# Order of the recurrence's activations, place of one projection, and the first two weights' loading in a two-layer trunk

## The chip, the cores and the metric

The kernel runs on one core of a Trainium2 chip. The metric is the time of one execution on the device, in microseconds. The engines of the core work side by side, each through its own queue in order: TensorE (PE; its weight loads PEld), VectorE (DVE), ScalarE (ACT), GpSimd (POOL), and SyncE (SP), which issues the transfers.

## What is computed

A trunk of two layers over 1024 latent tokens (x) and 256 context tokens, 1024 channels wide. The change touches the first layer only: its modulated input, the recurrence (RG-LRU) and the neighbouring gating unit. In the reference:

```python
shift, scale, gate = modulation(c, w_mod[l], b_mod[l])
h = x * (1.0 + scale) + shift
p = h @ w_in                       # five branches of 512 channels
xl = depthwise_conv(p[..., :W], conv_w, conv_b)
...
gate_r = sigmoid(einsum(xh, w_a) + b_a)      # for each of two directions
gate_i = sigmoid(einsum(xh, w_x) + b_x)
log_a = (-LRU_C * gate_r) * softplus(-lam)
a = exp(log_a)
bterm = sqrt(-expm1(2.0 * log_a)) * (gate_i * xc)
h_lat = linear_scan(a, b, forward) + linear_scan(a, b, reverse)
...
y_a = h_rec * silu(p[..., W:2 * W])
u = gelu(p[..., 2 * W:3 * W])
v = gelu(p[..., 3 * W:4 * W])
y_b = spatial_gating(u, v, ...) * silu(p[..., 4 * W:5 * W])
```

Everything is float32. Each matrix product is made of three matmuls on a high part and a low part of both operands: high by high, high by low, low by high.

## The kernel before

**Layout.** Channels lie on the partitions, tokens along the free dimension: 256 context and 1024 latent tokens, 1280 columns, in chunks of 256, 512 and 512. A weight tile has 128 output channels and eight blocks of 128 input channels. `wload` (line 143) fetches it into `wraw` (two buffers) and makes it into two halves of four blocks: `whi`, a ScalarE copy (L138), and `wlo`, a subtraction (L141), on GpSimd unless another engine is named; `whi` and `wlo` have four buffers each.

**The front (lines 264 to 338).** In eight steps of 128 input channels, `load0` fetches a block of x (640 KB) and of the modulation's weights (1 MB), four buffers each; `mod0` computes the modulation on TensorE (`modp`, L221), `hmod` transposes it (L298), scales x on VectorE (L307) and splits it into high parts (`hhc` for context, `hhl` for latents, L309, ScalarE) and low parts (`hlc`, `hll`, L312 and L313, VectorE). In between, step by step, TensorE advances two projections: `px` (weight 0, the recurrence's input of tile 0) and `pg` (weight 4, its gate branch), nine matmuls per step each (L164). The first four steps use the first half of each weight, the last four the second.

**The recurrence (lines 344 to 516).** The 512 channels of the recurrence are four tiles f = 0 to 3. For each: `lru_x` projects (`px`), evacuates it on ScalarE (`xp`, L363 and L364), convolves on VectorE (L367 and L369) and splits the result (`xh`, `xo`); `lru_g` projects (`pg`), takes a tanh on ScalarE (`sg`, L382) and multiplies on VectorE (L383), which reads `pg` in PSUM too; `lru_rec` computes four gates, two for each direction d, nine matmuls each (`pgate`, L399 to L401), a tanh of each (`gt`, L403: r, then x), a second tanh on r (`tt`, L407), Exp (L408), and four VectorE passes (L409 to L412); `lru_scan` takes Sqrt on ScalarE (L421), multiplies (L424), scans (L426 to L432), adds and gates (L438, L439) and stores the tile. The order of the calls is x0, g0, x1, then rec0 with scan0, g1, x2, rec1 with scan1, g2, x3, rec2 with scan2, g3, the u projection (`pu`, weight 8, with a Gelu into `ut0`, L513), rec3, the rest of the modulation blocks, and after that scan3, the z projection (`pz`, L530 and L531), a second u projection and the v tiles (`pv`, L208).

**PSUM.** All projections and gates take tiles of three banks from one tag with two buffers (`pj3`, line 260). A tile can therefore start only when all readers of the one before the last are done: for `px` that is ScalarE, for a gate its tanh, for `pg` the tanh and L383, for `pu` the Gelu, for `pz` L531.

**Order.** TensorE runs in program order. On the other engines a planner places the instructions: at each moment, of those that are ready, the one that comes first in the program. In the front, SyncE too runs in program order. `mod_step` (line 484) is called at several places; each third call does one block of modulation work (`mod_do`: 16 matmuls, a VectorE copy of its result, and, of the block before, a transpose or a gate row).

Of the kernel before, what the change touches and what calls it, by code (L numbers as in the profile page):

```python
# [10 lines left out]
F32 = mybir.dt.float32  # L11
F32R = mybir.dt.float32r
# [30 lines left out]
def tile_hybrid_trunk(es: ExitStack, tc: tile.TileContext, A, out, scr=None):  # L43
    nc = tc.nc
    V, S, G, T, SY = nc.vector, nc.scalar, nc.gpsimd, nc.tensor, nc.sync

    def pool(name, space=None, **kw):
        if space is not None:
            kw["space"] = space
        return tc.tile_pool(name=name, bufs=1, reuse_waits="tile", **kw)  # L50

    def f32(ap):
        return ap.bitcast(F32)
# [3 lines left out]
    wp = es.enter_context(pool("w"))  # L57
# [71 lines left out]
    def hs(c0, n):  # L129
        if c0 < CTX:  # L130
            return hhc[:, :, c0:c0 + n], hlc[:, :, c0:c0 + n]
        return hhl[:, :, c0 - CTX:c0 - CTX + n], hll[:, :, c0 - CTX:c0 - CTX + n]

    def split(hi, lo, src, he=None, le=None):
        he = he or S
        le = le or V
        if he is S:
            S.activation(hi, src, AF.Copy)  # L138
        else:
            he.tensor_copy(hi, src)  # L140
        le.tensor_tensor(lo, src, f32(hi), op=ALU.subtract)  # L141

    def wload(src, nk=8, le=None):
        raw = wp.tile([128, nk, 128], F32, name="wraw", tag="wraw", bufs=2)
        SY.dma_start(raw, src)
        res = []
        for h in range(nk // 4):
            hi = wp.tile([128, 4, 128], F32R, name="whi", tag="whi", bufs=4)
            lo = wp.tile([128, 4, 128], F32R, name="wlo", tag="wlo", bufs=4)
            split(hi, lo, raw[:, 4 * h:4 * h + 4], le=le or G)  # L150
            res.append((hi, lo))
        return res
# [5 lines left out]
    def proj3_g(ps, w):  # L158
        outs = [(ps[:, 256 + c0:256 + c0 + n], hs(c0, n)) for c0, n in CHUNKS]
        for k in range(KT):  # L160
            hi, lo = w[k // 4]
            for wt, hx, st, sp_ in ((hi, 0, k == 0, False), (hi, 1, False, False), (lo, 0, False, k == KT - 1)):
                for o, hh in outs:
                    T.matmul(o, wt[:, k % 4], hh[hx][:, k], start=st, stop=sp_)  # L164
            yield 1.63
# [11 lines left out]
    def proj3(ps, w):  # L177
        run(proj3c_g(ps, w))
# [81 lines left out]
    def pj3(name):  # L260
        t = pj.tile([128, 1536], F32, name=name, tag="pj", bufs=2)
        return t

    px0, pg0 = pj3("px"), pj3("pg")
# [8 lines left out]
    def load0(k):  # L273
        wm = stp.tile([128, KT, 256], F32, name="wm0", tag="wm0", bufs=4)
        xt = stp.tile([128, NTOK], F32, name="xt", tag="xt", bufs=4)
        if k:
            SY.dma_start(xt, A["xcT"][128 * k:128 * k + 128])
        if k:
            SY.dma_start(wm, A["w_mod0"][k])
        else:  # L280
            SY.dma_start(wm[:, 0:4], A["w_mod0"][k][:, 0:4])
            SY.dma_start(wm[:, 4:8], A["w_mod0"][k][:, 4:8])
            SY.dma_start(ident, A["ident"])
            SY.dma_start(xt, A["xcT"][128 * k:128 * k + 128])
        WM[k], XT[k] = wm, xt

    def mod0(k):
        p = psb("modp")
        wm = WM.pop(k)
        mod_mm(p[:, 0:256], [wm[:, i] for i in range(KT)], range(KT))  # L290
        mb = stp.tile([128, 256], F32, name="mb0", tag="mb0", bufs=2)
        S.activation(mb, p[:, 0:256], AF.Copy)
        return mb

    def hmod(k, mb):
        p = psb("modcp")
        for i in range(2):
            T.transpose(p[:, 128 * i:128 * i + 128], mb[:, 128 * i:128 * i + 128], ident)  # L298
        t = const.tile([128, 2, 2], F32, name="mct0", tag="mct", bufs=2)
        V.tensor_reduce(t, p[:, 0:256].rearrange("p (i g r) -> p i r g", g=4, r=32)[:, :, 0:2, :], axis=AX.X,  # L300
                        op=ALU.add)
        V.tensor_tensor(modc[:, k], t, bmodc[:, k, :, None].to_broadcast([128, 2, 2]), op=ALU.add)
        xt = XT.pop(k)
        parts = []
        for c0, n, cnd in ((0, 256, 1), (256, 512, 0), (768, 512, 0)):
            x = xt[:, c0:c0 + n]
            V.tensor_scalar(x, x, modc[:, k, 1, cnd:cnd + 1], modc[:, k, 0, cnd:cnd + 1], op0=ALU.mult, op1=ALU.add)  # L307
            hh, hl_ = hs(c0, n)
            S.activation(hh[:, k], x, AF.Copy)  # L309
            parts.append((hl_[:, k], x, f32(hh[:, k])))  # L310
            if len(parts) == 2:
                V.tensor_tensor(*parts.pop(0), op=ALU.subtract)  # L312
        V.tensor_tensor(*parts.pop(0), op=ALU.subtract)  # L313

    so_cm = tc.manual_schedule(engines={nc.sync.engine})
    so_cm.__enter__()
    load0(0)
    gx = proj3_g(px0, wload(A["w_in0"][0]))
    load0(1)
    gg = proj3_g(pg0, wload(A["w_in0"][4]))  # L320
    hmod(0, mod0(0))
    for k in range(KT):
        if k + 2 < KT:
            load0(k + 2)
        if k == 0:
            next(gx)
        if k == 3:
            decay()
        if k + 1 < KT:
            mb = mod0(k + 1)  # L330
        if k:
            next(gx)
        if k + 1 < KT:
            hmod(k + 1, mb)
        next(gg)
# [10 lines left out]
    with pool("lrua") as lp, pool("lruc") as lc:  # L346
        def lt(name, tag, bufs, dt=F32):
            t = {"gr": lb, "gx": lb, "tt": lb, "xl": lc}.get(tag, lp).tile([128, WC], dt, name=name, tag=tag, bufs=bufs)
            return t
# [36 lines left out]
        def lru_rec(f):  # L386
            (wh, wl), = wload(A["wg"][f], nk=4)
            mod_step()
            xl, xh, xo = XL[f]
            bs = []  # L390
            for d in range(2):
                i8 = 4 * d + f
                gts = []
                for g in range(2):
                    p = pj3("pgate")
                    m = 2 * d + g
                    for c0, n in ((0, 258), (258, 512), (770, 512)):
                        o = p[:, 254 + c0:254 + c0 + n]
                        T.matmul(o, wh[:, m], xh[:, c0:c0 + n], start=True, stop=False)  # L399
                        T.matmul(o, wh[:, m], xo[:, c0:c0 + n], start=False, stop=False)  # L400
                        T.matmul(o, wl[:, m], xh[:, c0:c0 + n], start=False, stop=True)  # L401
                    t = lt("gt", "gr" if g == 0 else "gx", 2)
                    S.activation(t, p[:, 254:1536], AF.Tanh, scale=0.5, bias=hb[:, 8 * g + i8:8 * g + i8 + 1])  # L403
                    gts.append(t)
                r, gi = gts
                tt = lt("tt", "tt", 2)
                S.activation(tt, r, AF.Tanh, scale=sp2[:, i8:i8 + 1], bias=sp2[:, i8:i8 + 1])  # L407
                S.activation(r, r, AF.Exp, scale=sn4[:, i8:i8 + 1], bias=sn4[:, i8:i8 + 1])  # L408
                V.scalar_tensor_tensor(gi, gi, 1.0, xl, op0=ALU.add, op1=ALU.mult)  # L409
                V.scalar_tensor_tensor(tt, r, 1.0, tt, op0=ALU.add, op1=ALU.mult)  # L410
                V.tensor_scalar(r, tt, -1.0, 1.0, op0=ALU.mult, op1=ALU.add)
                V.scalar_tensor_tensor(tt, r, 1.0, tt, op0=ALU.add, op1=ALU.mult)  # L412
                bs.append((r, gi, tt))
                mod_step()
            return bs

        def lru_scan(f, bs):
# [36 lines left out]
        def mod_do():  # L454
            if late:
                mod_c(*late.pop(0))
            if pend:
                l, blk, wm = pend.pop(0)
                p = psb("modp")
                mod_mm(p, wm, range(8))  # L460
                mb = lp.tile([128, 512], F32, name="mb", tag="mb", bufs=1)
                V.tensor_copy(mb, p)
                late.append((l, blk, mb))
                mod_load()
# [17 lines left out]
        late, pend, calls = [], [], [0]  # L482

        def mod_step():
            calls[0] += 1
            if calls[0] % 3 == 2:
                mod_do()
# [20 lines left out]
        u0 = u0_cm.__enter__()  # L508
        ut0 = u0.tile([128, NTOK], F32, name="ut0")
        zt0 = u0.tile([128, NTOK], F32, name="zt0")  # L510
        p = pj3("pu")
        proj3(p, wload(A["w_in0"][8]))
        S.activation(ut0, p[:, 256:1536], AF.Gelu_apprx_tanh)  # L513
        rec3 = lru_rec(3)
        while pend or late:
            mod_do()


    vp_cm = pool("sguv", side="right")
# [598 lines left out]
    with pool("out1") as op, pool("po1", PSUM) as po:  # L1118
        rows = []
        for i, nm in enumerate(("ln_g", "ln_b")):  # L1120
            for l in range(2):
                r = op.tile([128, D], F32, name=f"row{nm}{l}")
# [144 lines left out]
```

## Time and profile before

| | |
|---|---|
| median of three runs | 1149.4 us (1149.16 to 1150.6) |
| the profiled execution: its time | 1150.2 us |
| its span, first to last instruction | 1148.4 us |
| TensorE busy | 1122.0 us, 98% of the span |
| VectorE busy | 726.5 us, 63% |
| ScalarE busy | 448.8 us, 39% |
| GpSimd busy | 257.9 us, 22% |

All times in a trace count from the start of the span. In the order of time a line has the start, the duration, engine, source line, operation, output <- inputs, shapes and count; several like instructions in a row are merged (x2). Brackets hold the engine's idle time before it and what ended that. TensorE's matmuls overlap, and their ends are modelled, so that steps from start to start tell more than durations. The line of a helper (L138, L141) stands for whoever called it; the tile's name tells which.

### The profile page before, as it was taken

The numbers are of one execution on the slowest core, as the hardware profiler recorded it, in microseconds if no ns is written. First come the engines' busy times: TensorE is split into PE (matmuls) and PEld (weight loads), VectorE is DVE, ScalarE is ACT, GpSimd is POOL, SyncE is SP. The second block draws the span as 40 slices with busy tenths as digits, with TensorE's granted clock in tenths as the row PEclk, the third lists the DMA queues.
The fourth block names the chain that finished last, engine by engine and source line by source line (L and its number), as shares of the span: only waits on it lengthen the run. The fifth ranks groups of instructions, "written<-read, shape, count | busy, mean of one in ns | idle before, by whom it ended". The sixth has DMA issues, their size and how long they took to land. (4 is left out here: it accounts for less than half of the span.)

```text
span 1148.4 us, 14901 instructions
## 1 busy us (share of the span) xinstructions
PE 1122.0 (98%) x5842; PEld 922.1 (80%) x5842; DVE 726.5 (63%) x1025; ACT 448.8 (39%) x701; POOL 257.9 (22%) x176
## 2 busy tenths in 40 slices
PE   6999999999999999999999999999999999999997
PEld 3777777778888888888888788888888888888786
DVE  4678986943511566646302758876877876738996
ACT  3453755710131233352113545545554554423210
POOL 1022212540140122285301301122211211220021
PEclk9999999999999999999999999999999999999999
DMA  9554543230142544345215312332321410126641
GB/s 372 210 176 172 190 141 132 93 96 1 60 146 75 170 140 136 109 141 168 97 46 144 106 46 69 83 103 64 92 60 38 137 52 20 46 68 240 206 147 74
DMA packets 71093, 133.92 MB, mean 117 GB/s; under 512 B 5856, under 2 KB 34400, under 8 KB 70128
## 3 DMA queue, kind: packets, MB, share of 16 engines
q1 hardware_dynamic: 71024, 132.97, 34.4%
q8 instruction: 46, 0.75, 0.3%
q14 instruction: 23, 0.19, 0.0%
HBM read 105.67 MB, written 27.28 MB: 116 GB/s over the span
## 5 line engine op out<-in xcount | busy, mean ns | idle before, releaser
L141 POOL TENSOR_TENSOR wlo<-wraw,whi 128x512 fp32r<-128x512 f32 x90 | 137.8, 1536 | 561.1 <-ACT whi L138 561.1
L978 DVE TENSOR_REDUCE st<-psc 128x1 f32<-128x1280 f32 x64 | 95.1, 1485 | 36.9 <-PE psc L977 36.8
L661 PE MATMUL pout<-woh,yhi 128*128 128x512 f32 (+1 forms) x296 | 114.8, 388 | 0.3 <-DVE xres L1159 0.3
L663 PE MATMUL pout<-woh,ylo 128*128 128x512 f32 (+1 forms) x296 | 114.4, 386 | 0.3 <-DVE ylo L141 0.3
L980 ACT ACTIVATE e<-psc,st 128x1280 f32<-128x1280 f32 x64 | 85.1, 1330 | 75.1 <-DVE st L978 74.4
L662 PE MATMUL pout<-wol,yhi 128*128 128x512 f32 (+1 forms) x296 | 114.1, 386 | 0.0
L138 ACT ACTIVATE whi<-wraw 128x512 fp32r<-128x512 f32 x92 | 57.2, 628 | 126.3 <-PE px L173 29.0
L184 PE MATMUL p<-hhl,whi 128*128 128x512 f32 x256 | 104.7, 409 | 0.0
L186 PE MATMUL p<-hhl,wlo 128*128 128x512 f32 x256 | 100.6, 393 | 0.0
L185 PE MATMUL p<-hll,whi 128*128 128x512 f32 x256 | 100.3, 392 | 0.0
L976 PE MATMUL psc<-k,qh 128*128 128x512 f32 (+1 forms) x192 | 67.3, 365 | 2.1 <-ACT e L980 2.0
L977 PE MATMUL psc<-k,ql 128*128 128x512 f32 (+1 forms) x192 | 68.7, 358 | 0.0
L138 ACT ACTIVATE ah<-atr 128x512 fp32r<-128x512 f32 (+1 forms) x96 | 46.9, 523 | 50.1 <-PE atr L999 49.5
L661 PEld LDWEIGHTS pout<-woh,yhi 128*128 128x128 f32 x296 | 55.6, 188 | 12.4 <-issue 0.6
L663 PEld LDWEIGHTS pout<-woh,ylo 128*128 128x128 f32 x296 | 55.6, 188 | 12.0 <-DVE ylo L141 0.7
L138 ACT ACTIVATE yhi<-yraw 128x512 fp32r<-128x512 f32 x36 | 22.5, 631 | 109.0 <-PE pout L662 77.4
L662 PEld LDWEIGHTS pout<-wol,yhi 128*128 128x128 f32 x296 | 55.7, 188 | 11.6 <-DVE wol L141 0.2
L141 DVE TENSOR_TENSOR al<-atr,ah 128x512 fp32r<-128x512 f32 (+1 forms) x96 | 54.6, 594 | 6.4 <-ACT ah L138 6.0
L186 PEld LDWEIGHTS p<-hhl,wlo 128*128 128x128 f32 x256 | 48.0, 188 | 10.7
L185 PEld LDWEIGHTS p<-hll,whi 128*128 128x128 f32 x256 | 48.3, 189 | 8.4
L184 PEld LDWEIGHTS p<-hhl,whi 128*128 128x128 f32 x256 | 48.2, 188 | 8.3
L1081 DVE SCALAR_TENSOR_TENSOR e<-e,st 128x1280 f32<-128x1280 f32 x32 | 51.6, 1612 | 0.8
(320 smaller groups left out, 2813.1 us busy)
## 6 DMA issues: line engine op xcount, KB each, us to landing
wraw<-in_w_in_dram SPq DMA_DIRECT2D x44, 512.0 KB, 3.7
wm<-in_w_mod_dram SPq DMA_DIRECT2D x64, 256.0 KB, 4.6
wraw<-in_w_out_dram SPq DMA_DIRECT2D x16, 512.0 KB, 3.5
wm<-in_w_mod_dram SPq DMA_DIRECT2D x7, 1024.0 KB
xt<-in_xcT_dram SPq DMA_DIRECT2D x8, 640.0 KB, 10.1
xres<-in_xc_dram SPq DMA_DIRECT2D x10, 512.0 KB, 3.7
kd<-k_d SPq DMA_DIRECT2D x16, 320.0 KB, 4.8
wvr<-in_w_v_dram SPq DMA_DIRECT2D x8, 512.0 KB, 4.9
```

The lines of the kernel that those rows point to most:

```text
L138: S.activation(hi, src, AF.Copy)
L141: le.tensor_tensor(lo, src, f32(hi), op=ALU.subtract)
L184: T.matmul(o, hi[:, k % 4], hh[:, k], start=k == 0, stop=False)
L185: T.matmul(o, hi[:, k % 4], hl_[:, k], start=False, stop=False)
L186: T.matmul(o, lo[:, k % 4], hh[:, k], start=False, stop=k == KT - 1)
L661: T.matmul(o, hi[:, i], wh[:, c], start=first and i == 0, stop=False)
L662: T.matmul(o, hi[:, i], wl[:, c], start=False, stop=False)
L663: T.matmul(o, lo[:, i], wh[:, c], start=False, stop=not first and i == 3)
L976: T.matmul(o, qh[:, m, cu], KS[m][:, c:c + n], start=True, stop=False)
L977: T.matmul(o, ql[:, m, cu], KS[m][:, c:c + n], start=False, stop=True)
L978: V.tensor_reduce(st[:, m:m + 1], p[:, 256:1536], axis=AX.X, op=ALU.max, negate=True)
L980: S.activation(e_, p[:, 256:1536], AF.Exp, bias=st[:, m:m + 1], scale=1.0, accum_out=st[:, 2 + m:3 + m])
```

## The change

Three edits:

1. In `lru_rec` the four gates of a tile, for both directions, come first, each with its tanh; the second tanh, Exp and VectorE's passes follow for both directions. `mod_step` is called after each direction's gates; the order on TensorE within a tile is the same.
2. The first u projection (weight 8, 72 matmuls, its Gelu) comes after the gates of tile 3 and after the last modulation work, and no longer between g3 and rec3. So rec3 follows g3 directly.
3. The first two weights (0 and 4) are fetched in halves: the first half in the old place, the second half of weight 0 in step 1 and that of weight 4 in step 2. Their low parts are computed on VectorE (the default of `split`), not on GpSimd.

```diff
@@ -314,12 +314,32 @@
 
     so_cm = tc.manual_schedule(engines={nc.sync.engine})
     so_cm.__enter__()
+    def wstart(f):
+        raw = wp.tile([128, 8, 128], F32, name="wraw", tag="wraw", bufs=2)
+        res = []
+
+        def half(h):
+            SY.dma_start(raw[:, 4 * h:4 * h + 4], A["w_in0"][f][:, 4 * h:4 * h + 4])
+            hi = wp.tile([128, 4, 128], F32R, name="whi", tag="whi", bufs=4)
+            lo = wp.tile([128, 4, 128], F32R, name="wlo", tag="wlo", bufs=4)
+            split(hi, lo, raw[:, 4 * h:4 * h + 4])
+            res.append((hi, lo))
+
+        half(0)
+        return res, half
+
     load0(0)
-    gx = proj3_g(px0, wload(A["w_in0"][0]))
+    w0, half0 = wstart(0)
+    gx = proj3_g(px0, w0)
     load0(1)
-    gg = proj3_g(pg0, wload(A["w_in0"][4]))
+    w4, half4 = wstart(4)
+    gg = proj3_g(pg0, w4)
     hmod(0, mod0(0))
     for k in range(KT):
+        if k == 1:
+            half0(1)
+        if k == 2:
+            half4(1)
         if k + 2 < KT:
             load0(k + 2)
         if k == 0:
@@ -387,7 +407,7 @@
             (wh, wl), = wload(A["wg"][f], nk=4)
             mod_step()
             xl, xh, xo = XL[f]
-            bs = []
+            bs, gates2 = [], []
             for d in range(2):
                 i8 = 4 * d + f
                 gts = []
@@ -402,7 +422,11 @@
                     t = lt("gt", "gr" if g == 0 else "gx", 2)
                     S.activation(t, p[:, 254:1536], AF.Tanh, scale=0.5, bias=hb[:, 8 * g + i8:8 * g + i8 + 1])
                     gts.append(t)
-                r, gi = gts
+                gates2.append(gts)
+                mod_step()
+            for d in range(2):
+                i8 = 4 * d + f
+                r, gi = gates2[d]
                 tt = lt("tt", "tt", 2)
                 S.activation(tt, r, AF.Tanh, scale=sp2[:, i8:i8 + 1], bias=sp2[:, i8:i8 + 1])
                 S.activation(r, r, AF.Exp, scale=sn4[:, i8:i8 + 1], bias=sn4[:, i8:i8 + 1])
@@ -411,7 +435,6 @@
                 V.tensor_scalar(r, tt, -1.0, 1.0, op0=ALU.mult, op1=ALU.add)
                 V.scalar_tensor_tensor(tt, r, 1.0, tt, op0=ALU.add, op1=ALU.mult)
                 bs.append((r, gi, tt))
-                mod_step()
             return bs
 
         def lru_scan(f, bs):
@@ -508,12 +531,12 @@
         u0 = u0_cm.__enter__()
         ut0 = u0.tile([128, NTOK], F32, name="ut0")
         zt0 = u0.tile([128, NTOK], F32, name="zt0")
+        rec3 = lru_rec(3)
+        while pend or late:
+            mod_do()
         p = pj3("pu")
         proj3(p, wload(A["w_in0"][8]))
         S.activation(ut0, p[:, 256:1536], AF.Gelu_apprx_tanh)
-        rec3 = lru_rec(3)
-        while pend or late:
-            mod_do()
 
 
     vp_cm = pool("sguv", side="right")
```

## Rows read from the trace of the kernel before

**Rows 1.** The page: busy time, share of the span, instructions of each engine.

```profile
PE 1122.0 (98%) x5842; PEld 922.1 (80%) x5842; DVE 726.5 (63%) x1025; ACT 448.8 (39%) x701; POOL 257.9 (22%) x176
```

**Rows 2.** TensorE's waits: us in total, times, longest.

```profile
PE pgate L399 <- ACT ut L513: 1.3, 1, 1.3
...
PE pgate L399 <- ACT gt L403: 1.0, 2, 0.6
...
PE pv L208 <- DVE zt L531: 0.6, 1, 0.6
...
PE pg L172 <- ACT gt L403: 0.5, 1, 0.5
```

**Rows 3.** Order of time, 10 to 27 us: start, duration, what [idle before].

```profile
10.77 1.13 ACT L138 ACTIVATE whi<-wraw 128x512 fp32r<-128x512 f32 x2
11.24 0.42 DVE L312 TENSOR_TENSOR hlc<-xt,hhc 128x256 fp32r<-128x256 f32 x1
...
11.43 0.58 PE L164 MATMUL px<-hhc,whi 128*128 128x256 f32 x1 [2.04 <-ACT whi L138]
11.46 3.02 POOL L141 TENSOR_TENSOR wlo<-wraw,whi 128x512 fp32r<-128x512 f32 x2 [11.02 <-ACT whi L138]
...
13.26 1.76 DVE L313 TENSOR_TENSOR hll<-xt,hhl 128x512 fp32r<-128x512 f32 x1
...
16.87 1.94 PE L221 MATMUL modp<-wm,csil 128*32 128x256 f32 x16
...
20.01 1.05 PE L164 MATMUL pg<-hhl,whi 128*128 128x512 f32 x2
...
22.62 0.68 DVE L313 TENSOR_TENSOR hll<-xt,hhl 128x512 fp32r<-128x512 f32 x1
...
24.51 0.63 PE L164 MATMUL px<-hhl,whi 128*128 128x512 f32 x2
...
26.55 0.17 DVE L300 TENSOR_REDUCE mct<-modcp 128x4 f32<-128x16 f32 x1 [3.25 <-PE modcp L298]
```

**Rows 4.** Order of time on TensorE around gates, tiles 0 and 3.

```profile
73.11 0.29 PE L399 MATMUL pgate<-xh,whi 128*128 128x258 f32 x1
...
75.00 0.39 PE L399 MATMUL pgate<-xh,whi 128*128 128x258 f32 x1
...
196.91 0.39 PE L401 MATMUL pgate<-xh,wlo 128*128 128x512 f32 x1
198.63 0.39 PE L399 MATMUL pgate<-xh,whi 128*128 128x258 f32 x1 [1.33 <-ACT ut L513]
```

**Rows 5.** Order of time, TensorE and VectorE, where pg ends (three tiles).

```profile
97.64 0.28 PE L172 MATMUL px<-hhc,whi 128*128 128x256 f32 x1
...
102.05 1.46 DVE L383 SCALAR_TENSOR_TENSOR sg<-sg,pg 128x1280 f32<-128x1280 f32 x1
...
140.37 0.28 PE L172 MATMUL px<-hhc,whi 128*128 128x256 f32 x1
...
146.34 1.48 DVE L383 SCALAR_TENSOR_TENSOR sg<-sg,pg 128x1280 f32<-128x1280 f32 x1
...
181.63 0.28 PE L172 MATMUL pu<-hhc,whi 128*128 128x256 f32 x1
...
189.75 1.48 DVE L383 SCALAR_TENSOR_TENSOR sg<-sg,pg 128x1280 f32<-128x1280 f32 x1
```

**Rows 6.** Order of time on ScalarE, recurrence of tile 2.

```profile
159.94 1.47 ACT L407 ACTIVATE tt<-gt,sp 128x1282 f32<-128x1282 f32 x1
161.31 1.31 ACT L403 ACTIVATE gt<-pgate,hb 128x1282 f32<-128x1282 f32 x1
...
172.03 1.28 ACT L408 ACT_TABLE_LOAD   x1
...
182.62 1.28 ACT L421 ACTIVATE tt<-tt 128x1282 f32<-128x1282 f32 x1 [1.76 <-DVE tt L412]
...
185.73 1.24 ACT L382 ACTIVATE sg<-pg 128x1280 f32<-128x1280 f32 x1
```

## The prediction

> **What bounds the kernel now.** I read the page first: TensorE is busy for 98% of the span [rows 1]. Only two things can therefore change the time: idle time of TensorE, and stretches in which it runs slowly. The second view is the list of TensorE's waits [rows 2]. In the parts that the change touches it holds small sums: 1.3 us for a gate's matmuls that wait for the Gelu of the u projection, 1.0 us in two waits for a gate's tanh, 0.5 us for the next projection behind a tanh, 0.6 us for the v tiles behind a VectorE pass. The third view is the order of time in the first 27 us [rows 3]. There TensorE waits and also runs slowly: two 512-column matmuls take 1.05 us at 20.01, but 0.63 us at 24.51. [...] From 24 us on it has hardly a gap. So the whole matter is some 9 us at the front and five small waits in the recurrence.
>
> The matmuls' ends are modelled, so a listed gap is a little short. [...] The loss is 1.72 - 0.23 = 1.49, not the 1.33 of the bracket. I add the same 0.16 to every gap of that kind.
>
> **The front.** Before, ScalarE copies both halves of the first weight, 1.13 us for two, ahead of the latent columns; GpSimd computes both lows in 3.02 us; beside it VectorE's second subtraction (hll) takes 1.76 us, whereas the same pass takes 0.68 us at 22.62 with GpSimd idle [rows 3]. TensorE starts the first projection at 11.43 and reaches the next modulation only at 16.87. After: only one copy stands ahead, so the copies of the latent columns start 0.57 earlier, at 11.25, and the first of them is there at 11.8. VectorE is through with x when hlc starts, at 11.24; then one low (0.68, as the pass of the same size at 22.62), hlc 0.42 and two hll at 0.68 end at about 13.8. TensorE's nine matmuls of the first step need 3 x (0.21 + 2 x 0.427) = 3.2 us from 11.43 on, 0.21 being half of 0.427 for the 256 columns; they wait some 0.3 us for the copy and 0.4 us for the second hll: the modulation at 15.3 instead of 16.87, **-1.6 us**. Ends: -0.6, if only the copy counts, and -2.0, if neither wait is left.
>
> What is put later: the two second halves, each with a transfer, a copy and a VectorE low. The transfers stand on SyncE's queue ahead of what waits for free buffers, and the same bytes come in the end. VectorE idles 3.25 us per step while it waits for the transposes [rows 3], and four lows are 4 x 0.68. I take 0; if that cover failed each time, +2.7. A ScalarE copy whose transfer is late would hold the next modulation's copy behind it on the queue; that lies inside the same bound.
>
> **The tanh ahead.** No instruction is added or removed; the program order of ScalarE changes, and the planner places what is ready. In tile 2 the order was tanh of r, the second tanh on r (159.94), tanh of x (161.31), although x came first in the program too [rows 6]. It filled the time in which the gate's matmuls (75.00 - 73.11 = 1.89 us per gate [rows 4]) were not done. That filler stays ready after the change, so I expect the waits for the x tanh, 1.0 in the list [rows 2], to stay: between 0 and -1.3 with the 0.16 each, taken as 0. Between the third tanh and the second, Exp (L408) no longer has precedence. The next projection waited for that third tanh; its 0.54 + 0.16 goes: **-0.70** (0 if Exp still slips in).
>
> **The u projection behind the last gates.** The matmuls are the same 72, with one weight transfer, two copies, two GpSimd lows and a Gelu. It is moved past a gate weight's transfer, 36 gate matmuls, the last modulation steps, and on SyncE past their small transfers; the weights are fetched two tiles ahead in either order, so I cost the queues at 0. It no longer stands between gates that want its buffer: **-1.49**. The pass that the v tiles waited for (L531) stood behind the last tile's scans on VectorE; these now come a whole projection earlier: 0.62 + 0.16, **-0.78** (0 if the pass stays late). The last modulation's gate row still has two gates' matmuls ahead of it to cover VectorE's copy; if a scan stands in front of that copy, up to +2.4, taken as 0.
>
> **What takes its place.** The projections and gates share two PSUM buffers. The gates of the last tile now follow the pg projection directly. Their first gate takes the other buffer; the second wants pg's own, and this is free only when ScalarE's tanh (sg) and then VectorE's L383 have read it. Before, 72 matmuls of another projection covered that. The rows give the time from the start of the next tile on TensorE to the end of L383 [rows 5]: 102.05 + 1.46 - 97.64 = 5.87; 146.34 + 1.48 - 140.37 = 7.45; and for this very tile 189.75 + 1.48 - 181.63 = 9.60. One gate covers 1.89, so the stall is 3.98, 5.56 or 7.71 us. It cannot be below a table load, sg and L383, 1.28 + 1.24 + 1.48 [rows 6, 5], 4.1 with handoffs, less 1.89: 2.2 us. I take the mean of the first two, **+4.77**: in the third, the second Exp was kept behind a Sqrt and a further table load (172.03), so that the second Sqrt came at 182.62 [rows 6]; with both Exp closer together that should be less frequent. Behind the stalled matmuls stand the last modulation, two gates and all that follows; nothing else is there for TensorE to do.
>
> [...]
>
> **Sum.** -1.6 - 0.70 - 1.49 - 0.78 + 4.77 = +0.2 us. The profiled execution took 1150.2 us (span 1148.4 and 1.8 around it), 0.8 above the median of 1149.4; I put the difference on the median: **1149.6 us**. A measurement here tells a difference of about 0.2%, 2.3 us, from none.
>
> **The rivals.**
> 1. L383 slips in early. VectorE's scans depend on one another, and at 102.05 L383 went between others of its chain. With the floor of 2.2 and both x waits gone too (-1.3): -1.6 - 0.70 - 1.49 - 0.78 - 1.3 + 2.2 = -3.7, 1145.7 us. For it: 5.87 in tile 1, and an earlier Sqrt. Against it: 7.45 and 9.60 in the two tiles after.
> 2. Slower: VectorE's queue keeps L383 behind the whole scan of tile 2, as this tile's own row shows: +7.71 - 4.57 = +3.1, 1152.5 us. For it: VectorE is nearly full here, and TensorE arrives 0.7 us earlier. It decides from 8.8 us between the end of pg and the end of L383 (stall 6.9). Against it: the repeated table loads may go.
> 3. The clock's rise does not move with the work. Then the 1.6 us that come earlier are done at half pace and give back half: -0.8 instead of -1.6, +1.0 in all, 1150.4 us. The runs before lie 1.4 us apart, which would fit a rise that is not tied to the work.
> [...]
> 4. The change doesn't do what it says: the planner keeps ScalarE's order, Exp ahead of the third tanh. Then 0.70 is not won: +0.9, 1150.3 us, inside the forecast's own range.
>
> **How the numbers follow.** Chances: forecast with rival 4, 0.33; rival 3, 0.15; these two differ from before by less than 2.3 us. Rival 1 or a milder form of it with over 2.3 us: 0.26. Rival 2, or several of the costs put at 0: 0.26. So faster 0.26, same 0.48, slower 0.26. The likeliest case has a range of its own, 1147.3 to 1151.7. The range for 8 in 10 reaches to both rivals and a little past the slower one for the costs put at 0: 1145.8 to 1153.4.
>
> **What the profile of the changed kernel would show.** Right: the modulation that started at 16.87 near 15.3; no wait of a gate for the Gelu; none of the v tiles for L531; and a new wait of 4 to 6 us in the list, the last tile's second gate behind VectorE's L383. Wrong: a stall there under 2.5 or over 7 us; a projection that waits for a tanh again; ScalarE or VectorE waiting for a late weight half in the first 30 us; a rise of TensorE's pace at another time. The prediction falls if the second gate can start without L383, or if the planner's new order shifts waits in the attention part, which I leave out.

## The result, and the profile after

The changed kernel takes 1158.77 us (median of 6 runs, 1154.83 to 1160.58) against 1149.68 of the kernel before on the same chip: a ratio of 1.0076, with a 95% interval of 1.006 to 1.0093. The forecast was 1149.6 us with a range up to 1153.4; the change is 9 us slower. Line numbers after are 20 to 23 higher than before: the gates are L419 to L421, their tanh L423, the sg tanh and its VectorE pass L402 and L403 (before L382 and L383), the reverse scan L455, the output projection L684 to L686.

The profiled execution took 1158.45 us, its span 1156.5 (before 1150.2 and 1148.4). The page's first part, TensorE busy in the same matmuls for nearly the same time as before [rows 1]:

```profile
PE 1122.6 (97%) x5842; PEld 923.1 (80%) x5842; DVE 727.3 (63%) x1029; ACT 448.0 (39%) x700; POOL 248.1 (21%) x172
```

TensorE's waits after (us in total, times, longest), to lay beside [rows 2]:

```profile
PE pgate L419 <- ACT gt L423: 8.4, 3, 7.4
...
PE pout L684 <- DVE zt L647: 2.8, 1, 2.8
...
PE pu L174 <- POOL wlo L141: 1.4, 1, 1.4
...
PE pg L172 <- ACT gt L423: 0.5, 1, 0.5
```

The waits for the Gelu and for VectorE's zt pass in front of the v tiles are gone, as forecast. The two short waits for a tanh and the projection's 0.5 are still there. New are one wait of 7.4 us for a gate's tanh, one of 2.8 at the first output projection and one of 1.4 for a low.

Where the difference arises is read from the starts of the same matmul in both traces:

| matmul | before, us | after, us | after - before |
|---|---|---|---|
| first gate of tile 0 | 73.11 | 69.69 | -3.42 |
| first matmul of the z projection behind the recurrence | 207.91 | 212.09 | +4.18 |
| first matmul of the second u projection | 221.77 | 225.83 | +4.06 |
| first v tile | 236.30 | 241.28 | +4.98 |
| first output projection | 370.64 | 378.52 | +7.88 |
| span | 1148.4 | 1156.5 | +8.1 |

So the front wins 3.4 us, the last tile's gates lose some 7.5, and 3.7 more are lost between 208 and 379 us, in a part that the change doesn't touch.

**The front.** Order of time on ScalarE, VectorE and TensorE, 10 to 19 us (start, duration), and one line of before that [rows 3] leaves out:

```profile
10.14 0.63 ACT L138 ACTIVATE whi<-wraw 128x512 fp32r<-128x512 f32 x1 [0.89 <-DMA wraw<-in_w_in_dram]
10.45 1.32 DVE L307 TENSOR_SCALAR xt<-xt,modc 128x256 f32<-128x256 f32 x3
10.89 0.42 ACT L309 ACTIVATE hhc<-xt 128x256 fp32r<-128x256 f32 x1
...
11.69 0.68 DVE L141 TENSOR_TENSOR wlo<-wraw,whi 128x512 fp32r<-128x512 f32 x1
...
13.23 0.69 DVE L313 TENSOR_TENSOR hll<-xt,hhl 128x512 fp32r<-128x512 f32 x1
...
15.76 1.46 PE L221 MATMUL modp<-wm,csil 128*32 128x256 f32 x16
...
18.14 0.62 PE L164 MATMUL pg<-hhl,whi 128*128 128x512 f32 x2
```

```profile
10.00 1.32 DVE L307 TENSOR_SCALAR xt<-xt,modc 128x256 f32<-128x256 f32 x3
```

Against [rows 3]: one ScalarE copy ahead of the latent columns instead of two, hll in 0.69 instead of 1.76 us, and the modulation at 15.76 instead of 16.87. In this execution VectorE's scaling of x (the x pass, L307) began 0.45 us later than before. From its start to the modulation it is 6.87 us before (10.00 to 16.87) and 5.31 after (10.45 to 15.76): 1.56 less, as forecast; the seven other traces with this front have 5.31 too, and the modulation at 15.27 to 15.43. The last row of after is a second thing: two 512-column matmuls of pg take 0.62 us at 18.14, where [rows 3] has 1.05 at 20.01. TensorE already has the faster pace; before, it came only between 20 and 24.5 us.

**The last tile's gates.** The same view, 178 to 191 us:

```profile
178.19 0.29 PE L419 MATMUL pgate<-xh,whi 128*128 128x258 f32 x1
...
179.73 0.39 PE L421 MATMUL pgate<-xh,wlo 128*128 128x512 f32 x1
187.51 0.58 PE L419 MATMUL pgate<-xh,whi 128*128 128x258 f32 x1 [7.38 <-ACT gt L423]
...
190.89 0.59 PE L497 MATMUL gatep<-mb,par 128*2 128x512 f32 x1
...
182.28 1.24 ACT L402 ACTIVATE sg<-pg 128x1280 f32<-128x1280 f32 x1
186.12 1.33 ACT L423 ACTIVATE gt<-pgate,hb 128x1282 f32<-128x1282 f32 x1 [2.61 <-DVE tt L455]
...
183.68 2.35 DVE L455 TENSOR_TENSOR_SCAN tt<-gt,tt 128x1024 f32<-128x1024 f32 x1
...
186.26 1.48 DVE L403 SCALAR_TENSOR_TENSOR sg<-sg,pg 128x1280 f32<-128x1280 f32 x1
```

From 179.73 to 187.51 with one step of 0.23 taken off, the stall is 7.55 us. It is not the wait that was forecast. The gate starts while L403, which frees the pg projection's buffer, has run for 1.25 of its 1.48 us: it doesn't want pg's buffer. In the built program's addresses the projections and gates alternate before between PSUM banks 2 to 4 and 5 to 7; after, both the first and the second gate of the last tile have banks 2 to 4. So the second gate waits for the first gate's own tanh. That tanh waits (2.61 us, in the bracket) for VectorE's reverse scan of tile 2, which reads the r that lies in the SBUF buffer that the tanh is to write. With pg's buffer it would have been no better: L403 ends at 187.74, 9.55 us after the gates' start at 178.19, and 9.55 - 1.89 = 7.66.

The stretch behind the stall, and one at the output projection (the column behind POOL is the granted clock):

```profile
core 0: us, PE busy (x) PEld busy (x) DVE busy (x) ACT busy (x) POOL busy (x), PEclk, DMA share, GB/s
178.00:186.00 8.00, 2.12 (x11) 1.48 (x9) 6.59 (x5) 4.31 (x4) 2.05 (x1) 0.87 0.20 66
186.00:190.00 4.00, 2.49 (x7) 2.15 (x8) 4.00 (x6) 2.36 (x2) 0.00 (x0) 0.50 0.02 4
190.00:192.00 2.00, 2.00 (x15) 0.77 (x17) 0.39 (x2) 1.97 (x3) 0.00 (x0) 0.83 0.59 229
378.00:382.00 4.00, 3.48 (x9) 2.77 (x10) 3.96 (x4) 0.83 (x1) 0.00 (x0) 0.57 0.29 123
```

The granted clock falls in the stall (0.87 on average from 178 to 186 us) and is 0.50 behind it: the second gate takes 190.89 - 187.51 = 3.38 us instead of the 1.89 of [rows 4], 1.49 more. Up to the z projection: -3.42 + 7.55 + 1.49 - 1.49 (the Gelu's wait) = +4.13, and +4.18 was read.

**Behind it.** 1.43 + 0.16 us are lost for a low that GpSimd delivers late, and some 0.7 won where the v tiles do not wait. Then comes the first output projection, 375 to 380 us on TensorE and VectorE, and under it the same place before:

```profile
375.28 0.39 PE L174 MATMUL pz<-hhl,wlo 128*128 128x512 f32 x1
378.52 0.80 PE L684 MATMUL pout<-woh,yhi 128*128 128x512 f32 x1 [2.85 <-DVE zt L647]
...
379.54 0.63 PE L686 MATMUL pout<-woh,ylo 128*128 128x512 f32 x1
...
376.98 1.49 DVE L647 SCALAR_TENSOR_TENSOR zt<-zt,pz 128x1280 f32<-128x1280 f32 x1 [12.24 <-ACT zt L646]
```

```profile
370.64 0.39 PE L661 MATMUL pout<-woh,yhi 128*128 128x512 f32 x1
...
372.11 1.49 DVE L624 SCALAR_TENSOR_TENSOR zt<-zt,pz 128x1280 f32<-128x1280 f32 x1 [12.25 <-ACT zt L623]
```

The output projection starts when VectorE has read the last z projection. Before, it started in the next step (370.64) though that same pass ran from 372.11 to 373.60. After the change the matmuls behind it step at 0.43 us, the slower pace again, with a granted clock of 0.57 from 378 to 382 us.

### The profile page after: what moved, and what is told of

It reads as the page before. It is cut to its first block, busy times and chain, and to the rows that moved or that the text cites. A ratio compares the mean times of both kernels' runs of the same rounds, so it can differ in the third digit from the quotient of the medians.

```text
span 1156.5 us, 14898 instructions
## 1 busy us (share of the span) xinstructions
PE 1122.6 (97%) x5842; PEld 923.1 (80%) x5842; DVE 727.3 (63%) x1029; ACT 448.0 (39%) x700; POOL 248.1 (21%) x172
## 5 line engine op out<-in xcount | busy, mean ns | idle before, releaser
L141 POOL TENSOR_TENSOR wlo<-wraw,whi 128x512 fp32r<-128x512 f32 x86 | 130.6, 1522 | 573.6 <-ACT whi L138 572.5
L684 PE MATMUL pout<-woh,yhi 128*128 128x512 f32 (+1 forms) x296 | 115.4, 390 | 2.8 <-DVE zt L647 2.8
L686 PE MATMUL pout<-woh,ylo 128*128 128x512 f32 (+1 forms) x296 | 114.9, 388 | 0.2 <-DVE ylo L141 0.2
L684 PEld LDWEIGHTS pout<-woh,yhi 128*128 128x128 f32 x296 | 56.0, 189 | 14.5 <-DVE zt L647 3.3
L686 PEld LDWEIGHTS pout<-woh,ylo 128*128 128x128 f32 x296 | 56.0, 189 | 12.1 <-DVE ylo L141 0.6
```

The costliest lines, as they stand in the source:

```text
L684: T.matmul(o, hi[:, i], wh[:, c], start=first and i == 0, stop=False)
L686: T.matmul(o, lo[:, i], wh[:, c], start=False, stop=not first and i == 3)
```

## The experiments

Each kernel was timed beside the kernel before on one chip. The medians of before lay between 1148.86 and 1149.68 us, so a difference between two of these kernels can carry some 0.8 us of that.

**The parts alone.** The first edit (the four tanh ahead) changes nothing: built by itself, on the kernel before or on the fastest variant below, it gives the same instructions in the same order on all five engines. The other two ran, first the front (the third edit, and nothing else of the change):

```diff
+    w0, half0 = wstart(0)
...
+    w4, half4 = wstart(4)
...
+            half0(1)
...
+            half4(1)
```

> The kernel before with the front part alone: the first and the fifth weight fetched in halves, their lows on VectorE. In the trace of the changed kernel TensorE stands 3.4 us earlier than before at 54 us, not the 1.6 us of the prediction. Theory 'the front gains all of this by itself and keeps it': 3.4 us below the kernel before, with the granted clock's rise near 16.6 us instead of 23.5. Rival 'the lead is given back in the recurrence, because VectorE and ScalarE are no earlier': 0 to 1.6 us below before, with new waits of TensorE between 60 and 190 us.

1146.4 us against 1148.99, a ratio of 0.9974 (0.9965 to 0.9984): -2.6 us, between the forecast's -1.6 and the -3.4 of the traces. Up to the end of the recurrence TensorE keeps a lead of 3 us over the trace of before, and no wait comes in its place.

The second edit alone, the move of the u projection:

```diff
+        rec3 = lru_rec(3)
+        while pend or late:
+            mod_do()
         p = pj3("pu")
         proj3(p, wload(A["w_in0"][8]))
         S.activation(ut0, p[:, 256:1536], AF.Gelu_apprx_tanh)
-        rec3 = lru_rec(3)
-        while pend or late:
-            mod_do()
```

> The kernel before with the u projection moved behind the last tile's gates, and nothing else. Theory 'the whole loss comes from the move': with the front's 3.4 us taken out of the changed kernel's +9, this kernel is 12 to 12.5 us slower than before, with the stall of some 7.5 us ahead of the last tile's second gate, a granted clock of 0.5 for some microseconds behind it, and the wait of 2.8 us at the first output projection tile. Rival 'the grouped tanh or the front share in the loss, by a different order of ScalarE in the last tile': under 10 us slower. The forecast's own step for the move, +4.77 - 1.49 - 0.78 = +2.5 us, would leave it at +2.5.

1157.88 us, 1.0088 (1.0067 to 1.011): +8.9, where I had expected 12 to 12.5 and the rival under 10; the interval, +7.7 to +12.6, holds both. The loss comes with the move, since the front alone gains and the first edit changes nothing. It has the same stall, here on TensorE:

```profile
189.16 0.58 PE L399 MATMUL pgate<-xh,whi 128*128 128x258 f32 x1 [7.40 <-ACT gt L403]
```

The wait of 2.8 us at the output projection is there too, but neither the late low of 1.4 us nor the lower clock behind the output's wait (1.00 from 375 to 385 us). The two parts make +6.3 together, the changed kernel +9.1. In its profiled execution those two are some 3 us (1.6 and 1.5); but neither is in every trace of the moved kernels, so for the medians it stays open whether they make the difference.

**What the second gate waits for.** The changed kernel with one more SBUF buffer for the tanh of r:

```diff
-                    t = lt("gt", "gr" if g == 0 else "gx", 2)
+                    t = lt("gt", "gr" if g == 0 else "gx", 3 if g == 0 else 2)
```

> The changed kernel with three SBUF buffers instead of two for the r gate's tanh (tag gr). Theory 'the second gate of the last tile waits because the tanh of its first gate waits for the SBUF buffer that the reverse scan of tile 2 still reads': the stall of 7.55 us shrinks to 5 us or less, the wait's releaser changes from that tanh to another, and if the stall gets short enough the granted clock does not fall at 184: 2.5 to 5 us less than the changed kernel. Rival 'the PSUM buffer held by the gate projection until its tanh and L403 have read it is what ends last' (the prediction's own mechanism): L403 began at 186.26 and ended at 187.74, so the stall stays at 7 us or more and the time stays within 1 us of the changed kernel's.

1154.52 us, 4.2 less than the changed kernel (+5.5 over before, not +9.1). TensorE, ScalarE and VectorE, and the clock behind it:

```profile
184.74 0.58 PE L419 MATMUL pgate<-xh,whi 128*128 128x258 f32 x1 [4.70 <-ACT gt L423]
...
183.36 1.32 ACT L423 ACTIVATE gt<-pgate,hb 128x1282 f32<-128x1282 f32 x1
...
186.22 1.48 DVE L403 SCALAR_TENSOR_TENSOR sg<-sg,pg 128x1280 f32<-128x1280 f32 x1
...
186.00:190.00 4.00, 4.00 (x18) 1.85 (x20) 4.00 (x5) 1.65 (x2) 0.00 (x0) 0.55 0.00 0
```

The tanh now follows sg directly, at 183.36, and the gate starts 1.48 us ahead of L403's start. The rival, which was the forecast's own mechanism, falls for this gate. What is left, 4.7 us, is ScalarE: the r tanh stands behind a Sqrt that waits 1.74 us for VectorE, a copy (0.61 us), a table load (1.28) and sg (1.24). The clock still falls, to 0.55.

**Why the output projection waits.** The last z projection lies after in banks 2 to 4 and the first output tile begins in bank 2; before it lay in banks 5 to 7. Three attempts to give them different banks:

```diff
+        pd = pj3("pdum")
+        T.transpose(pd[:, 0:128], onesm, ident)
         p = pj3("pu")
```

> The changed kernel with one further PSUM tile taken between the last modulation and the u projection (one small transpose into it, read by nobody), so that all later projections sit in the other one of the two buffers. Theory 'parity': in the changed kernel the second gate took its first gate's buffer again, so the last z projection sits in the buffer that the first output projection tile wants; with the further tile the wait of 2.8 us at 375.7 goes, and with it the half clock from 378.4 to 381.8: 4 to 4.3 us less than the changed kernel. Rival 'the wait at the output projection comes from VectorE being late there, whatever the buffer': the wait stays, and the time is the changed kernel's within 0.5 us (0.1 us for the transpose).

1158.41 us, with the wait still 2.85. In the built program the further tile took banks 5 to 7 and the u projection took them again: nothing was shifted.

```diff
-        out_mm(p, wo0, YA.pop(t) if t in YA else y_load(y0, ya_d, 128 * t, 2), 0, True)
+        out_mm(p, wo0, YA.pop(t) if t in YA else y_load(y0, ya_d, 128 * t, 2), 0, True,
+               halves=(0, 1) if t else (1, 0))
```

> The changed kernel, with the two column halves of the first output projection tile computed in the other order (second half first), so that its first 12 matmuls write another PSUM bank. In the changed kernel all pj tiles behind the last tile's second gate sit in the other one of the two buffers: the last z projection in banks 2 to 4, and the first output tile begins in bank 2. Theory 'the wait of 2.8 us at the first output projection is that bank': it goes (12 matmuls of 0.235 us cover it), 2.8 us less than the changed kernel, and up to 1.7 us more where the granted clock fell at 378 us. Rival 'VectorE or a late weight is what the output projection waits for': the wait stays under another name, same time as the changed kernel within 0.5 us.

1158.12 us, with the wait still 2.85. The tile that is written first got bank 2 whichever half it was. Both edits left the cause in place, so neither speaks against it; the third did shift it.

```diff
+    pd = po.tile([128, 512], F32, name="poutd", tag="pout", bufs=6)
+    V.memset(pd[:, 0:2], 0.0)
     out0_a(0)
```

> The changed kernel with one further PSUM tile in the output stage's pool (VectorE sets two columns of it, nobody reads it). By the built program this gives the first output projection tile bank 7 instead of bank 2, in which the last z projection lies; the edits of e7_parity and e8_halves10 left it in bank 2. Theory 'the wait of 2.8 us ahead of the first output projection is that bank': the wait goes, 2.8 us less than the changed kernel (up to 1.7 more where the granted clock fell there). Rival 'VectorE or a late weight': the wait stays, same time as the changed kernel within 0.5 us.

1154.72 us, 4.1 less than the changed kernel (+5.9 over before):

```profile
374.97 0.39 PE L684 MATMUL pout<-woh,yhi 128*128 128x512 f32 x1
...
376.44 1.49 DVE L647 SCALAR_TENSOR_TENSOR zt<-zt,pz 128x1280 f32<-128x1280 f32 x1 [12.25 <-ACT zt L646]
```

The projection starts 1.5 us ahead of the pass that it waited for. The wait is the bank, and the bank comes from one buffer handed out differently 190 us earlier.

**All losses taken away at once.** The third r buffer and the further output tile as above, and the last modulation between the last tile's first and second gate:

```diff
                     gts.append(t)
+                    if f == 3 and d == 0 and g == 0:
+                        mod_step()
                 gates2.append(gts)
-                mod_step()
+                if f != 3 or d:
+                    mod_step()
```

> The changed kernel with each named loss taken away: a third SBUF buffer for the tanh of r, the last tile's modulation step between its first and second gate, the further PSUM tile of e8b_bank7. Theory 'these are all the losses': the stall of 4.7 us that e5_gr3 left shrinks by the 2.7 us of the modulation to about 2 us, the granted clock does not fall at 184 us, the wait at 375 us is gone; with the Gelu's 1.49 and the v tiles' 0.78 won, the time is e1_front's 1146.4 + 2.0 - 1.5 - 0.8 = 1146.1 us, 1145 to 1148. Rival 'something else in the moved order costs': 1149 us or more. If the granted clock falls again for some 7 us although the stall is 2 us, 1.5 us more than the theory.

1149.72 us, 1.0008 (0.9998 to 1.0017): 9 us less than the changed kernel, not told apart from the kernel before, and 3.6 above the theory: the rival came true. The three gates behind the first on TensorE, a tanh on ScalarE, and the clock:

```profile
184.72 0.39 PE L419 MATMUL pgate<-xh,whi 128*128 128x258 f32 x1 [2.07 <-ACT gt L423]
187.73 0.39 PE L419 MATMUL pgate<-xh,whi 128*128 128x258 f32 x1 [0.98 <-DVE sg L403]
191.64 0.39 PE L419 MATMUL pgate<-xh,whi 128*128 128x258 f32 x1 [1.89 <-ACT gt L423]
...
188.91 1.46 ACT L434 ACTIVATE tt<-gt,sp 128x1282 f32<-128x1282 f32 x1 [4.25 <-DVE gt L464]
...
186.00:192.00 6.00, 3.12 (x16) 2.05 (x15) 5.85 (x8) 3.09 (x3) 0.00 (x0) 1.00 0.07 23
```

The first stall is 2.07, as expected, and the clock stays at 1.00. But the third gate now waits 0.98 for L403, the mechanism of the forecast, and the fourth 1.89 for a tanh behind another that waited 4.25 us for VectorE's add of tile 2. Together with 0.16 each these two make 3.2 us in this trace, near the 3.6. So the stall was not one wait: behind the pg projection TensorE outruns tile 2's scan on VectorE. With the r buffer out of the way, the next two that stand behind the scan show: pg's, and that of the second tanh.

**Where the front gains.** Halves with the lows on GpSimd, and whole fetches with the lows on VectorE:

```diff
-            split(hi, lo, raw[:, 4 * h:4 * h + 4])
+            split(hi, lo, raw[:, 4 * h:4 * h + 4], le=G)
```

> The front part alone as in e1_front, but with the lows of the halves on GpSimd. Theory 'the lows on VectorE are what gains, because VectorE's passes are slow beside GpSimd's': the second subtraction (hll) of the first step takes some 1.7 us again, only the second ScalarE copy of 0.57 us is saved, and the first step's modulation starts near 16.3 us: 0.6 to 1 us less than before. Rival 'the half fetch gains, whoever computes the low': modulation near 15.8 us as in the changed kernel, 2.6 us less than before as e1_front. The granted clock's rise (23.5, 16.6, 18.4 and 19.0 us in four traces so far) adds up to 1.6 us to either.

```diff
-    gx = proj3_g(px0, wload(A["w_in0"][0]))
+    gx = proj3_g(px0, wload(A["w_in0"][0], le=V))
-    gg = proj3_g(pg0, wload(A["w_in0"][4]))
+    gg = proj3_g(pg0, wload(A["w_in0"][4], le=V))
```

> The kernel before with the first and the fifth weight fetched whole, but their lows on VectorE instead of GpSimd. Theory 'the lows on VectorE are what gains': hll of the first step takes 0.68 instead of 1.76 us, against one or two more lows of 0.68 on VectorE in the first step: 1 to 2 us less than before. Rival 'the half fetch gains': both ScalarE copies still stand ahead of the latent columns, two more VectorE passes stand ahead of hll, TensorE reaches the first step's modulation at 16.9 us or later: within 0.5 us of before, or slower.

1147.63 us (0.9986, 0.9977 to 0.9996) and 1146.24 us (0.9969, 0.9957 to 0.9981): -1.7 and -3.1, beside -2.6 for the two together. Rows of the former, and in the second block of the latter:

```profile
10.00 2.27 DVE L307 TENSOR_SCALAR xt<-xt,modc 128x256 f32<-128x256 f32 x3
10.18 1.35 POOL L141 TENSOR_TENSOR wlo<-wraw,whi 128x512 fp32r<-128x512 f32 x1 [9.74 <-ACT whi L138]
...
13.13 0.68 DVE L313 TENSOR_TENSOR hll<-xt,hhl 128x512 fp32r<-128x512 f32 x1
...
15.76 1.07 PE L221 MATMUL modp<-wm,csil 128*32 128x256 f32 x16
```

```profile
10.19 1.32 DVE L307 TENSOR_SCALAR xt<-xt,modc 128x256 f32<-128x256 f32 x3
...
13.57 0.69 DVE L313 TENSOR_TENSOR hll<-xt,hhl 128x512 fp32r<-128x512 f32 x1
...
16.10 1.80 PE L221 MATMUL modp<-wm,csil 128*32 128x256 f32 x16
```

From the x pass to the first modulation it is 5.76 us with halves on GpSimd and 5.91 with whole fetches, against 6.87 before and 5.31 with both: each alone wins 1.1 and 1.0 us of the 1.6. The medians do not follow that order, and the two intervals overlap; the whole fetches' -3.1 is as large as the gain with halves, but the modulation's start does not account for it. Against my expectation hll is not slow with halves on GpSimd (0.68 us). GpSimd's low now runs from 10.18, and the x pass beside it takes 2.27 us instead of 1.32.

**Does the clock rise at a fixed place?** The kernel before once more.

> The kernel before once more, unchanged, for a second trace: does the granted clock rise at the same place of the program? If it is tied to the work, at 23.5 us as in the first trace. If not, somewhere between 15 and 23 us, as in the others, with up to 1.7 us less time: the front of e2_umove is the same program, and there it rose at 18.99.

1148.39 us. TensorE in its front and at its first v tile, and under it a row of the first trace of before:

```profile
16.82 1.94 PE L221 MATMUL modp<-wm,csil 128*32 128x256 f32 x16
...
19.96 1.04 PE L164 MATMUL pg<-hhl,whi 128*128 128x512 f32 x2
...
20.96 0.63 PE L164 MATMUL pg<-hll,whi 128*128 128x512 f32 x2
...
234.31 0.39 PE L208 MATMUL pv<-wvh,hhc 128*128 128x512 f32 x1
```

```profile
21.08 1.05 PE L164 MATMUL pg<-hll,whi 128*128 128x512 f32 x2
```

The same program as in [rows 3], the modulation at the same time (16.82), but the pace rises between 20 and 21 us (two matmuls in 1.04 us at 19.96, in 0.63 at 20.96), not after 22. In the trace with the moved u, whose front is also that of before, it does so ahead of 19.77. From there on this trace of before leads the first by 1.0 to 1.2 us, so against it the changed kernel's front leads by 2.2 us at the first gate of tile 0 (71.92 to 69.69), not 3.4. And its v tiles do not wait: the first matmul follows in the next step, 0.23 us, with no bracket, and the lead grows to 2.0. The wait of [rows 2] is thus not in every execution of the kernel before.

**The Gelu's wait in place.** The front alone, with the last modulation put between the last tile's first and second gate, and u where it was:

```diff
                     gts.append(t)
+                    if f == 3 and d == 0 and g == 0:
+                        mod_step()
                 r, gi = gts
...
-                mod_step()
+                if f != 3 or d:
+                    mod_step()
```

> The front part alone (e1_front), u projection in its old place, and the last tile's modulation step put between its first and its second gate instead of behind the second. Theory 'what the move of u was to win, the wait of 1.49 us of the second gate for the Gelu, can be covered in place, since 16 modulation matmuls take 2.7 us': the wait goes and nothing else comes: 1.5 us less than e1_front. Rival 'the wait only moves': the modulation then has to wait for its own data, or the gate behind it for the first gate's tanh; same time as e1_front within 0.5 us.

1145.8 us against 1149.32, 0.9968 (0.9957 to 0.998): the fastest kernel here, 3.5 us under the one before; it is only 0.6 under the front alone, with intervals that overlap. The second and the fourth gate on TensorE, and the table load on ScalarE between them:

```profile
196.02 0.39 PE L419 MATMUL pgate<-xh,whi 128*128 128x258 f32 x1
...
201.45 0.39 PE L419 MATMUL pgate<-xh,whi 128*128 128x258 f32 x1 [1.64 <-ACT gt L423]
...
197.43 1.28 ACT L430 ACT_TABLE_LOAD   x1
```

The Gelu's wait is gone, and the fourth gate waits 1.64 us for a tanh behind a table load and an Exp: the rival was right that the wait moves. From the first gate of tile 0 to the z projection this trace takes 135.04 us, that of the front alone 134.69: nothing is won there.

## Why the prediction was wrong

- **The step that failed** is "the second wants pg's own, and this is free only when ScalarE's tanh (sg) and then VectorE's L383 have read it", with its +4.77. The mechanism was wrong: I took the alternation of two buffers as a rule (before the prediction it stands as "all readers of the one before the last"). The gate got its predecessor's buffer, so it waited for a tanh that had an SBUF buffer of its own to wait for, held by tile 2's scan. The stall was 7.55.
- **The size failed at another place: "I take the mean of the first two".** This tile's own row, 9.60 us from the next tile's start to the end of L383, was set aside because "both Exp closer together" should help; the first edit changes no order, and after the change the same stretch is 9.55 us. So, by that trace, pg's own buffer would have cost 7.66: the wrong buffer alone hardly changes the time, the choice of the rows does, by 2.9. Rival 2 had this price (7.71) and its reason, L383 behind the whole scan of tile 2; that the gate did not wait for L383 escaped it too.
- **The price of a stall was taken as its length.** With it the granted clock fell to 0.50, 1.49 us more on the next gate. No row of before showed a stall of that length in the middle of the kernel, and I had set no bound for it.
- **What lies far behind was put at nothing.** "The prediction falls if ... the planner's new order shifts waits in the attention part, which I leave out": the shift came nearer, at the output projection of the first layer, 2.9 us, with 1.5 of lower clock behind it in this execution. One buffer handed out out of turn changed the bank of all the projections that follow.
- **The queues at 0.** The low of the second u projection came 1.4 us late from GpSimd (3.29 us for this one, behind six lows of the v weights). In the trace with the u move alone it cost nothing, nor in that of the second attempt at the banks, the same program up to there: the end of a margin, not a fixed price.
- **The front, -1.6**, was right in its means and in what it priced: 1.56 us less from the x pass to the modulation. What it lacked is the pace. 2.3 us more come in that execution from the earlier rise of the pace, and the medians give -2.6 for the part, beyond the ends that I gave (-0.6 to -2.0). Of the rivals, number 3, a rise that does not move with the work, is right in that three traces of one front rise at three places (23.5, 20.9 and 19.0 us). It was wrong about the sign, since in all ten traces with a changed front the pace rose earlier (15.5 to 18.4 us) than in the three without (19.0 to 23.5).
- **The steps in the sums**, 0.427 and 0.23 us, and the 0.16 on a bracket were right. In the trace of before the two 512-column matmuls at 20.01 take 0.85 us to the next start (20.86) and those at 24.51 take 0.47 (24.98): 0.427 and 0.235 us each. At the Gelu's wait there are 1.72 us from 196.91 to 198.63 [rows 4]; less one step of 0.23 that is 1.49, 0.16 more than the bracket's 1.33. The same 0.16 on the other brackets was an estimate from this one gap; read in the same way, the brackets of 0.39, 0.61, 0.54 and 0.62 us lack 0.15 to 0.17.
- **The tanh ahead, -0.70**: nothing, as in rival 4; the projection still waits 0.5 us. ScalarE's order is the planner's, which takes what is ready.
- **The Gelu, -1.49**: as forecast. **The v tiles, -0.78**: about 0.7 between the two traces compared, but that the move took it is not shown. Of the six traces with u in its old place three have the wait and three do not, the second one of before among these.

Of the signs that the prediction named for being wrong, these came: a stall over 7 us, a projection that waits for a tanh again, the pace's rise at another time, and a second gate that starts without L383.

Against the first trace of before, the sum with the sizes that were read is -3.4 - 1.49 - 0.7 + 7.55 + 1.49 + 1.6 + 2.9 + 1.5 = +9.4, which the traces show at 382 us; 1.3 of it is gone again by the end of the span, in many small differences that I have not followed.

Open stays why the pace rises earlier with the changed fronts, the halves on GpSimd among them, and why the clock fell at 378 us in two of the traces with the wait of 2.85 us there and not in three others.

## What to carry to other kernels

Work that stands between two stages, here a projection between pg and the gates, is also the time in which the slower engines empty every buffer that the next stage will write: before moving it, list each of these buffers, SBUF and PSUM, with the instruction that frees it, and not only the one that comes to mind. Look up in the built program which buffer a tile gets after the change; two buffers need not alternate, and one turn out of step can cost microseconds much later (here a wait of 2.85 us, 190 us on). Where a planner orders an engine by what is ready, a new order of the source may change nothing: compare the built orders before costing it. And where a row of the very place stands against two of others, set it aside only for a reason that has been seen to hold.

## What the hardware showed that I had not expected

- With stalls of 7.4 and 4.7 us of TensorE the granted clock fell to 0.50 to 0.55 for the next matmuls; with waits of 2.07, 0.98 and 1.89 us and work between them it did not (1.00). With a wait of 2.85 us it fell in two traces of five.
- The front's pace is not the program's alone: the same two 512-column matmuls took 1.05 us at 21.08 in one trace of before and 0.63 at 20.96 in the other.
- Beside GpSimd's low more of VectorE's work was slow than its subtractions: the x pass, which reads one tile, took 2.27 us there instead of 1.32. ScalarE's copy of the first latent columns (L309) waited 0.99 us for it and started at 11.85; with the low on VectorE behind the x pass (the front alone) it followed the copy before it without a wait, at 11.02. Why, no run here shows.
